# Modulation weighed row by row on VectorE with only partition sums on TensorE, the opening in quarters of 256 features, GpSimd out of both input projections

## Chip, cores and metric

One core of one Trainium2 chip. The metric is the device time of one execution in microseconds; the kernel before takes 3154.66 us (median of three runs, 3153.15 to 3156.14).

## What is computed

Two layers of a diffusion transformer with 1024 latent tokens and 256 context tokens, 1024 features, in f32.

```python
for l in range(DEPTH):                                   # DEPTH = 2
    sh1, sc1, g1, sh2, sc2, g2 = adaln(c, w_mod[l], b_mod[l])         # silu(c) @ w_mod + b_mod, six parts of 1024
    csh1, csc1, cg1, csh2, csc2, cg2 = adaln(c_ctx, w_mod[l], b_mod[l])
    h  = modulate(rms_norm(x, norm1_g[l]), sh1, sc1)                  # h * (1 + scale) + shift
    hc = modulate(rms_norm(xc, norm1_g[l]), csh1, csc1)
    q, k, v, up, ca, cb = project_inputs(h, w_in[l], ...)             # and the same of hc
    attn = diff_attn_post(diff_attention(q, k_all, v_all, lam), ...)  # 4 heads, keys of context and latents
    pool_o = pool_mixer(up, pool_w[l], pool_scale[l])
    conv_o = conformer_conv(ca, cb, ...)                              # depthwise, 31 taps
    mix = jnp.concatenate([attn, pool_o, conv_o], axis=-1)
    x = x + g1 * jnp.einsum('blm,md->bld', mix, w_out[l])
    x = x + g2 * swiglu(modulate(rms_norm(x, norm2_g[l]), sh2, sc2), w_ffn_in[l], w_ffn_out[l])
    if not last:
        xc = ...                                                      # the context, with its own modulation
```

## The kernel before

Features lie on the 128 partitions and tokens along the free dimension, in two blocks of 512 latent tokens and one of 256 context tokens. Every matmul operand is split into two parts (`hi`, rounded by ScalarE, and `lo`, the rest, by VectorE or GpSimd), and each product is three matmuls. `Stream` loads weight tiles ahead of their use and splits them; its argument `lo` says which engine makes the lower parts ("v" VectorE, "p" GpSimd), tile after tile.

A layer is an input projection (14 column tiles, then v), the attention, an output projection and a feed-forward. All DMAs of weights are issued from the SP queue. The order on each engine is that of emission: the main flow emits TensorE's products, and beside it "lanes" (`Kern.lane`) emit smaller work piece by piece, each at a time that a rough forecast (`Clock`) gives. A lane that yields "v-" goes on when the forecast has VectorE idle; so do the convolution's taps (`taps`, 30 adds per 128 channels, besides the centre). What is left of the taps when the attention begins goes on beside it.

The modulation (`adaln`) takes w_mod in tiles of 128 input rows by 512 outputs. Each tile is split, and two matmuls with four columns of the condition (both conditions, in two parts) as weights and the tile as the moving operand add a row of 512 outputs in PSUM; `adaln_end` turns the rows to columns. At the start the tiles of the parts 1 and 0 (scale and shift of the first norm) are loaded whole, every other one is used unsplit in f32, and nothing of the projection begins before both parts are complete. The other four parts of the first layer run on a lane beside the first projection with GpSimd's lower parts; the second layer's six run beside the first feed-forward. GpSimd also adds the squares of the norms (`sq_acc`), makes the pooling sums (`pool_mix`, `POOL_ENG`) and most lower parts of the projections' weights (`P1_LO`), and in the attention the difference of the two softmaxes (`C`).

In the profile, L165 is the line of `Eng` through which every instruction of VectorE, ScalarE, GpSimd and SP goes, and L272 and L277 are TensorE's `mm` and `transpose`; so rows are told apart by tiles: `half` and `part` are tiles of 512 columns, `big` of 1024, `bank` PSUM, `dww` the taps' weights, `mod` the modulation, `cond_st` and `cond_raw` the conditions split and whole, `p`, `st`, `S`, `at` the attention's.

## Time and profile before

| | us |
|---|---|
| median of three runs | 3154.66 |
| span of the profiled execution, first to last instruction | 3148.1 |
| TensorE busy | 2957.6 |
| VectorE busy | 1728.9 |
| GpSimd busy | 1135.8 |
| ScalarE busy | 1098.9 |

The profiled execution has its span alone; the runs' median lies 6.6 us above it. Busy times are unions over one engine's instructions; an engine's idle time counts only where another waits for it.

### The profile page before, as it was taken

How to read it: one execution, taken by the hardware profiler on the slowest of the kernel's cores; microseconds unless marked ns; L12 is line 12 of the kernel's file. 1: busy time of each engine (PE TensorE's matmuls, PEld its weight loads, DVE VectorE, ACT ScalarE, POOL GpSimd, SP SyncE). 2: the span in 40 equal slices, each digit the busy share in tenths (PEclk: the TensorE clock that was granted, in tenths of full speed). 3: DMA queues.
4: the chain of work that ended last, by engine and by line, in shares of the span. 5: the costliest groups of instructions: out<-in, count | busy, mean ns of one | idle time of the engine just before them, and what ended most of it. 6: DMA issues, size and time to landing. Idle time of an engine off the chain costs nothing.

```text
span 3148.1 us, 38069 instructions
## 1 busy us (share of the span) xinstructions
PE 2957.6 (94%) x14708; PEld 2408.0 (76%) x14708; DVE 1728.9 (55%) x2413; ACT 1098.9 (35%) x1892; POOL 1135.8 (36%) x914
## 2 busy tenths in 40 slices
PE   6868898999999999999999998899999999999999
PEld 2646677877777778888888877678877888888887
DVE  5998758985645454332333498869956222322223
ACT  5424536763423332222222233357744111111110
POOL 3655406871423223233332423318832212211221
PEclk9989898999999999999999999999999999999999
DMA  6324364326333232111111222283252111111111
GB/s 229 108 90 122 123 192 140 105 76 203 114 100 95 93 101 81 34 41 41 34 41 40 75 68 70 81 239 95 88 173 75 48 47 54 47 47 47 48 47 54
DMA packets 133188, 283.52 MB, mean 90 GB/s; under 512 B 13840, under 2 KB 47248, under 8 KB 133008
## 3 DMA queue, kind: packets, MB, share of 16 engines
q1 hardware_dynamic: 132720, 280.83, 28.3%
q8 instruction: 116, 1.90, 0.3%
q14 instruction: 64, 0.52, 0.1%
q10 hardware_dynamic: 288, 0.26, 0.0%
HBM read 231.75 MB, written 49.28 MB: 89 GB/s over the span
## 4 chain that ended last, share of the span: by engine, by line
PE 61%; DVE 8%; issue 2%; ACT 1%; POOL 1%; DMA 1%; SPq 0%; DVEq 0%; ACTq 0%; POOLq 0%
PE bank L272 59%; DVE big L165 4%; DVE st L165 2%; DVE half L165 1%; PE S L272 1%; PE bank L277 1%; DVE part L165 1%; DVE at L165 1%; ACT p L165 0%; ACT big L165 0%; POOL p L165 0%; DMA big<-QS 0%; POOL big L165 0%; ACT half L165 0%; DVE rn L165 0%
## 5 line engine op out<-in xcount | busy, mean ns | idle before, releaser
L272 PE MATMUL bank<-part,big 128*128 128x512 f32 (+1 forms) x7536 | 1625.7, 374 | 29.8 <-DVE part L165 9.0
L272 PEld LDWEIGHTS bank<-part,big 128*128 128x128 f32 x7536 | 1321.6, 191 | 310.3 <-DVE part L165 12.9
L165 POOL TENSOR_TENSOR big<-big,big 128x1024 fp32r<-128x1024 f32 (+2 forms) x177 | 431.7, 2450 | 1141.5 <-ACT big L165 850.0
L272 PE MATMUL bank<-half,big 128*128 128x512 f32 (+1 forms) x2640 | 564.5, 373 | 5.4 <-DVE big L165 2.1
L272 PEld LDWEIGHTS bank<-half,big 128*128 128x128 f32 x2640 | 460.0, 188 | 104.4 <-DVE big L165 4.5
L165 DVE TENSOR_TENSOR big<-big,bank 128x512 f32<-128x512 f32 (+1 forms) x130 | 82.7, 679 | 821.4 <-PE bank L272 450.2
L165 DVE SCALAR_TENSOR_TENSOR big<-bank,mod,big 128x512 f32<-128x512 f32 (+1 forms) x560 | 390.4, 736 | 149.9 <-PE bank L272 143.6
L165 ACT CAST big<-big 128x1024 fp32r<-128x1024 f32 (+2 forms) x322 | 298.4, 955 | 68.8 <-DVE big L165 29.8
L165 POOL TENSOR_TENSOR half<-half,half 128x512 fp32r<-128x512 f32 (+2 forms) x141 | 202.7, 1445 | 328.7 <-ACT half L165 298.3
L165 DVE TENSOR_TENSOR big<-big,big 128x1024 fp32r<-128x1024 f32 (+3 forms) x177 | 214.8, 1220 | 188.1 <-ACT big L165 175.4
L165 ACT ACTIVATE big<-bank 128x512 f32<-128x512 f32 x88 | 48.1, 595 | 607.4 <-PE bank L272 607.4
L165 POOL TENSOR_TENSOR big<-big,half 128x256 f32<-128x256 f32 x160 | 124.7, 780 | 289.4 <-ACT half L165 289.4
L165 POOL TENSOR_TENSOR p<-p,p 128x512 f32<-128x512 f32 (+1 forms) x200 | 221.1, 1105 | 16.7
L165 ACT ACTIVATE half<-bank,mod 128x256 f32<-128x256 f32 x160 | 75.8, 474 | 375.1 <-PE bank L272 375.1
L165 DVE TENSOR_REDUCE st<-S 128x1 f32<-128x1280 f32 (+1 forms) x144 | 195.8, 1362 | 12.3 <-PE S L272 12.3
L165 DVE SCALAR_TENSOR_TENSOR big<-big,dww,big 128x1009 f32<-128x1009 f32 (+14 forms) x120 | 200.2, 1701 | 0.5
L165 POOL TENSOR_SCALAR p<-p,st 128x512 f32<-128x512 f32 (+1 forms) x200 | 123.3, 616 | 192.9 <-DVE st L165 150.7
L165 ACT ACTIVATE p<-S,st 128x1280 f32<-128x1280 f32 (+1 forms) x144 | 177.7, 1234 | 39.7 <-DVE st L165 38.0
L272 PE MATMUL S<-kv,big 128*128 128x512 f32 (+1 forms) x672 | 157.7, 370 | 9.6 <-ACT p L165 6.1
L272 PEld LDWEIGHTS S<-kv,big 128*128 128x128 f32 x672 | 120.1, 191 | 37.7 <-ACT p L165 12.3
L272 PE MATMUL bank<-at,kv 128*128 128x256 f32 x960 | 137.5, 290 | 0.0
L165 DVE TENSOR_TENSOR at<-bank,at 128x512 fp32r<-128x512 f32 (+1 forms) x200 | 115.7, 588 | 29.2 <-ACT at L165 25.0
(107 smaller groups left out, 2364.9 us busy)
## 6 DMA issues: line engine op xcount, KB each, us to landing
big<-in_w_ffn_in SPq DMA_DIRECT2D x88, 512.0 KB, 3.6
big<-in_w_mod SPq DMA_DIRECT2D x48, 512.0 KB, 3.8
big<-in_w_ffn_out SPq DMA_DIRECT2D x44, 512.0 KB, 3.7
big<-in_w_out SPq DMA_DIRECT2D x40, 512.0 KB, 4.9
half<-in_w_mod SPq DMA_DIRECT2D x64, 256.0 KB, 3.5
big<-QS SPq DMA_DIRECT2D x128, 128.0 KB, 5.3
big<-in_w_in SPq DMA_DIRECT2D x28, 512.0 KB, 4.8
VS<-big SPq DMA_DIRECT2D x40, 256.0 KB, 3.6
```

The source lines that it names most:

```text
L165: r = fn(*a, **k)
L272: self.tc.nc.tensor.matmul(out, lhsT, rhs, start=start, stop=stop)
L277: self.tc.nc.tensor.transpose(out, in_, ident)
```

## The change

- Modulation: each row of a w_mod tile is multiplied by its condition value (a scalar per partition) and added up over the eight tiles on VectorE in f32 (`weigh`; the first tile of eight on ScalarE); four matmuls with a single column of ones then sum over the partitions and leave columns at once (`column_sums`). The tiles are not split. This holds for both conditions in the parts 4, 3, 5 of the first layer and 1, 0 of the second, for the latents' condition alone in the second layer's other four, and in the opening. Part 2 of the first layer stays with `adaln`.
- Opening: shift and scale come in four quarters of 256 features each. A quarter's tiles hold both (two pieces of 256 columns per row). Once a quarter is weighed, its two feature tiles of the first block are normed, and their products with the four gated column tiles go out, before the next quarter. The context's condition uses f32 matmuls on the same tiles (`open_rows`); quarters 2 and 3 are loaded a second time for it.
- GpSimd: `P1_LO` is ("v",), `POOL_ENG` is "v", and `sq_acc` adds on VectorE.
- Parts 4, 3, 5 of the first layer go from the lane beside the first projection to one that begins with the output projection.

```diff
-P1_LO = ("v", "p", "v") + ("p",) * 11
+P1_LO = ("v",)
-POOL_ENG = "p"
+POOL_ENG = "v"
...
+    def weigh(self, acc, w, k, j):
+        c = self.c4[:, k, j:j + 1]
+        if k == 0:
+            self.act(acc, w, AF.Identity, scale=c)
+        else:
+            self.nc.vector.scalar_tensor_tensor(acc, w, c, acc, ALU.mult, ALU.add)
+
+    def column_sums(self, ps, accs):
+        for j, acc in enumerate(accs):
+            for c in range(4):
+                self.mm(ps[:, 4 * j + c:4 * j + c + 1], acc[:, c * P:c * P + P], self.one, True, True)
...
+    def adaln_v(self, l, chunk, conds, pace, ne=2):
+        st = Stream(self, self.mod_aps(l, [chunk], ne), new=self.half if ne == 1 else self.big, raw_ahead=1)
+        m = self.cp.tile([P, 2, 8], F32, name=self.name("mod"))
+        for n in range(2):
+            accs = [self.half() for _ in range(conds)]
+            for kk in range(KD // ne):
+                w = st.get_raw(KD // ne * n + kk)
+                for e in range(ne):
+                    for j in range(conds):
+                        self.weigh(accs[j], w[:, e, :], ne * kk + e, j)
+                yield pace * ne / 2
+            yield self.pe(*accs)
+            ps = self.bank2()
+            self.column_sums(ps, accs)
...
     def sq_acc(self, acc, x, first):
...
-            self.nc.gpsimd.tensor_tensor(acc, acc, t, ALU.add)
+            self.nc.vector.tensor_tensor(acc, acc, t, ALU.add)
...
-        for _ in self.adaln(0, [1, 0], 0.0, ne=1, whole=True, raw_ahead=RAW):
-            self.adv()
-        self.finish("norm0", "mod")
+        weigh(0, range(KD))
+        ps = columns(0)
+        rows(0)
+        loads(2)
+        weigh(1, range(2))
+        normed(0, ps)
+        ws += [st_in.get(x, 0) for x in range(2)]
+        weigh(1, range(2, KD))
+        ws += [st_in.get(x, 0) for x in range(2, GATED)]
+        outs += [self.bank() for _ in range(GATED)]
+        ps = columns(1)
+        products(0)
+        rows(1)
...
-        self.lane("ada", self.adaln(0, [2, 4, 3, 5], 3.0, ne=1, split_ahead=1, raw_ahead=1, lo=("p",)), ADA_AT)
+            self.lane("ada", self.adaln(0, [2], 3.0, ne=1, split_ahead=1, raw_ahead=1), ADA_AT)
...
+            if not last:
+                for chunk in (4, 3, 5):
+                    self.lane("ada", self.adaln_v(l, chunk, 2, 3.5, ne=1))
...
-            self.lane("ada", self.adaln(l + 1, [1, 0, 2, 4, 3, 5], 5.0, split_ahead=0, raw_ahead=1))
+            for chunk in (1, 0, 2, 4, 3, 5):
+                self.lane("ada", self.adaln_v(l + 1, chunk, 2 if chunk < 2 else 1, 12.0))
```

How the instructions stand now is shown at three places. First GpSimd, from the opening's square sums (`half_133`) to the first projection; before, the squares of the second block and the context and weights' and modulation's lower parts follow:

```order
L165 TENSOR_TENSOR half_133<-half_133,half_155 128x512
L165 TENSOR_TENSOR big_446<-big_443,big_445 128x1024
L165 TENSOR_TENSOR half_134<-half_134,half_473 128x512
L165 TENSOR_TENSOR half_134<-half_134,half_480 128x512
L165 TENSOR_TENSOR half_134<-half_134,half_483 128x512
```

Now, from its constants to the attention's first softmax difference (`p`), GpSimd has only this:

```order
masks.py:199 AFFINE_SELECT ident<-ident 128x128
L163 MEMSET big_1225 128x8 x2
L163 MEMSET big_1230 128x8 x2
L163 MEMSET big_2012 128x8 x2
L163 MEMSET big_2017 128x8 x2
L163 TENSOR_SCALAR p_3143<-p_3143,st_3134 128x256
```

Second VectorE in the opening. Before, the last part of the modulation (`mod_310` is the shift, `mod_158` the scale) stands ahead of the first instruction of the norm (`half_465`):

```order
L165 TENSOR_TENSOR mod_310<-bank_112_390,params 128x2x4
L165 TENSOR_TENSOR mod_310<-bank_112_390,mod_310 128x2x4
L165 TENSOR_TENSOR big_440<-big_437,big_439 128x1024
L165 SCALAR_TENSOR_TENSOR half_465<-big_116,mod_158,half_306 128x512
L165 SCALAR_TENSOR_TENSOR half_468<-big_117,mod_158,half_306 128x512
L165 SCALAR_TENSOR_TENSOR part_405<-half_465,mod_310,part_397 128x512
```

Now the first norm (`half_290`, with the scale `mod_134`) stands behind the first quarter's sums and one weighing of the second quarter (`half_284`), and two weight tiles are split (`big_299`, `big_303`) before the weighing goes on:

```order
L163 SCALAR_TENSOR_TENSOR half_284<-part_202,cond_raw,half_284 128x512
L163 TENSOR_TENSOR mod_133<-bank_62_244,params 128x2
L163 TENSOR_TENSOR mod_134<-bank_62_244,params 128x2
L163 SCALAR_TENSOR_TENSOR mod_134<-mod_134,params 128x2
L163 SCALAR_TENSOR_TENSOR half_290<-big_116,mod_134,half_233 128x512
L163 SCALAR_TENSOR_TENSOR half_293<-big_117,mod_134,half_233 128x512
L163 SCALAR_TENSOR_TENSOR part_168<-half_290,mod_133,part_160 128x512
L163 SCALAR_TENSOR_TENSOR part_169<-half_293,mod_133,part_161 128x512
L163 TENSOR_TENSOR big_299<-big_192,big_298 128x1024
L163 TENSOR_TENSOR big_303<-big_194,big_302 128x1024
L163 SCALAR_TENSOR_TENSOR half_284<-part_204,cond_raw,half_284 128x512
```

Third VectorE in the first attention, between the same two maxima (`TENSOR_REDUCE`) of scores in `S`. Before:

```order
L165 TENSOR_TENSOR big_4346<-big_4104,big_4346 128x256
L165 TENSOR_REDUCE st_4366<-S_4401 128x1
L165 TENSOR_TENSOR at_4409<-bank_1491_4410,at_4408 128x4x128
L165 SCALAR_TENSOR_TENSOR r_1405_3968<-r_1405_3968 128x4
L165 TENSOR_REDUCE st_4445<-S_4433 128x1
L165 TENSOR_TENSOR at_4375<-bank_1495_4440,at_4374 128x4x128
L165 SCALAR_TENSOR_TENSOR rn_4454<-bank_1497_4449,r_1405_3968 128x4
```

Now, with the convolution's taps (`dww`) and the sums and differences of its closing norm (`big_3868`, `big_821`, `big_923`) among them:

```order
L163 TENSOR_TENSOR big_3771<-big_3522,big_3771 128x256
L163 SCALAR_TENSOR_TENSOR big_614<-big_614,dww_597 128x242
L163 SCALAR_TENSOR_TENSOR big_923<-big_622,dww_597,big_923 128x1009
L163 TENSOR_REDUCE st_3791<-S_3826 128x1
L163 TENSOR_TENSOR at_3836<-bank_1115_3837,at_3835 128x4x128
L163 SCALAR_TENSOR_TENSOR r_1018_3385<-r_1018_3385 128x4
L163 SCALAR_TENSOR_TENSOR big_614<-big_614,dww_597 128x241
L163 TENSOR_TENSOR big_3868<-big_821,big_923 128x512
L163 TENSOR_SCALAR big_614<-big_614,dww_597,params 128x256
L163 SCALAR_TENSOR_TENSOR big_614<-big_614,dww_597 128x241
L163 TENSOR_REDUCE st_3877<-S_3860 128x1
```

In the first attention VectorE has 400 instructions between the first and the last matmul with `S`, where it had 321; in the second 281, where it had 253.

## Rows read from the trace of the kernel before

**Rows 1.** The page's first part: the span, then for each engine its busy time in us, its share of the span and its number of instructions.
```profile
span 3148.1 us, 38069 instructions
PE 2957.6 (94%) x14708; PEld 2408.0 (76%) x14708; DVE 1728.9 (55%) x2413; ACT 1098.9 (35%) x1892; POOL 1135.8 (36%) x914
```

**Rows 2.** Busy time by stage: the stretch in us from the span's start and its length, then the busy us and instructions of TensorE, of its weight loads, of VectorE, ScalarE and GpSimd, the clock granted to TensorE (1 is full), the share of the DMA engines and GB/s. The stretches are the opening, the first input projection, the first attention, the first output projection, the first feed-forward, the second projection and the second attention.
```profile
0.00:48.00 48.00, 28.57 (x92) 5.81 (x92) 19.34 (x41) 22.46 (x38) 12.67 (x14) 0.98 0.96 343
48.00:456.00 408.00, 333.88 (x1570) 257.42 (x1571) 337.47 (x439) 167.94 (x322) 191.94 (x119) 0.90 0.37 116
456.00:701.00 245.00, 221.18 (x1397) 192.95 (x1396) 206.33 (x344) 170.18 (x331) 175.73 (x208) 0.94 0.38 110
701.00:838.00 137.00, 127.38 (x644) 105.08 (x642) 75.53 (x87) 53.17 (x75) 42.62 (x28) 0.99 0.55 184
838.00:1809.00 971.00, 966.79 (x4924) 796.41 (x4925) 400.88 (x571) 269.00 (x448) 294.20 (x236) 1.00 0.21 65
1809.00:2104.00 295.00, 261.03 (x1238) 213.45 (x1236) 245.72 (x318) 110.21 (x200) 76.28 (x38) 0.95 0.33 104
2104.00:2301.00 197.00, 182.96 (x1217) 160.61 (x1218) 180.07 (x268) 147.96 (x263) 163.21 (x189) 1.00 0.35 102
```

**Rows 3.** What TensorE waited for from 48 to 456 us: the waiting engine, tile and line, the releaser, us in total, number of waits, the longest.
```profile
PE bank L272 <- DVE big L165: 37.1, 8, 25.8
```

**Rows 4.** The timeline of GpSimd and VectorE from 49 us on: start, length, engine, line, operation, tiles, shapes, number merged into the row.
```profile
49.79 11.65 POOL L165 TENSOR_TENSOR half<-half,half 128x512 f32<-128x512 f32 x7 [3.09 <-ACT half L165]
50.09 1.78 DVE L165 SCALAR_TENSOR_TENSOR half<-big,mod,half 128x512 f32<-128x512 f32 x1
...
62.58 0.74 DVE L165 SCALAR_TENSOR_TENSOR half<-big,mod,half 128x512 f32<-128x512 f32 x1
```

**Rows 5.** The convolution's taps over the whole span, long ones (latent tokens) and short ones (context), by the tile that holds their weights: minimum, median and maximum duration in ns, first and last start.
```profile
L165 DVE SCALAR_TENSOR_TENSOR big<-big,dww,big x120: 1251/1272/3431, 111.9 to 2024.7; 128x1009 f32<-128x1009 f32 x8, 128x1010 f32<-128x1010 f32 x8, 128x1011 f32<-128x1011 f32 x8, 128x1012 f32<-128x1012 f32 x8
L165 DVE SCALAR_TENSOR_TENSOR big<-big,dww x60: 461/474/2610, 143.0 to 436.4; 128x241 f32<-128x241 f32 x4, 128x242 f32<-128x242 f32 x4, 128x243 f32<-128x243 f32 x4, 128x244 f32<-128x244 f32 x4
```

**Rows 6.** The timeline of VectorE and, below it, of GpSimd around 1890 us, in the second projection: runs of long taps, the first without work on GpSimd until 1886.
```profile
1878.76 9.58 DVE L165 SCALAR_TENSOR_TENSOR big<-big,dww,big 128x1018 f32<-128x1018 f32 x8
1888.47 26.20 DVE L165 SCALAR_TENSOR_TENSOR big<-big,dww,big 128x1022 f32<-128x1022 f32 x12
...
1896.57 9.87 POOL L165 TENSOR_TENSOR big<-big,big 128x1024 f32<-128x1024 f32 x3
```

**Rows 7.** Busy time of VectorE in the two projections, of instructions on the taps' weights alone.
```profile
48.00:456.00 408.00, 158.78 (x126) 0.90 0.37 116
1809.00:2104.00 295.00, 93.31 (x62) 0.95 0.33 104
```

**Rows 8.** Groups of instructions from 48 to 456 us, by shape: number, busy us and mean ns of one, then idle time before them; two of GpSimd, one of VectorE.
```profile
L165 POOL TENSOR_TENSOR half<-half,half 128x512 fp32r<-128x512 f32 x64 | 108.5, 1712 | 115.6 <-ACT half L165 89.2 <-DVE big L165 7.2 <-ACT rn L165 6.5
L165 POOL TENSOR_TENSOR big<-big,big 128x1024 fp32r<-128x1024 f32 x13 | 33.5, 2583 | 31.0 <-ACT big L165 23.0 <-issue 7.9
...
L165 DVE TENSOR_TENSOR big<-big 128x512 f32<-128x512 f32 x10 | 13.5, 1365 | 14.6 <-ACT big L165 14.6
```

**Rows 9.** The same kinds on VectorE where GpSimd does nothing: two groups from 2050 to 2100 us, and a single split of 1024 columns at 43 us (a timeline's row).
```profile
L165 DVE SCALAR_TENSOR_TENSOR big<-big,ls,big 128x512 f32<-128x512 f32 x4 | 3.0, 742 | 0.0
L165 DVE TENSOR_TENSOR big<-big 128x512 f32<-128x512 f32 x2 | 1.4, 686 | 0.7 <-ACT big L165 0.7
...
43.28 1.22 DVE L165 TENSOR_TENSOR big<-big,big 128x1024 fp32r<-128x1024 f32 x1
```

**Rows 10.** TensorE's timeline at two places where it doesn't pause: four matmuls of the modulation, and a sum over partitions (four calls), each with the row behind it.
```profile
859.51 1.08 PE L272 MATMUL bank<-big,cond_st 128*4 128x512 f32 x4
860.43 0.75 PE L272 MATMUL bank<-part,big 128*128 128x256 f32 x5
...
755.10 0.95 PE L272 MATMUL bank<-ones,half 128*128 128x1 f32 x8
755.91 1.40 PE L272 MATMUL bank<-part,big 128*128 128x512 f32 x5
```

**Rows 11.** Busy time in two shorter stretches, the middle of the first attention and the first part of the first feed-forward (columns as in rows 2).
```profile
550.00:650.00 100.00, 96.37 (x650) 85.30 (x649) 93.66 (x144) 76.79 (x139) 84.42 (x98) 1.00 0.39 117
840.00:1250.00 410.00, 407.74 (x2067) 323.02 (x2066) 206.44 (x274) 137.97 (x214) 114.16 (x87) 1.00 0.31 94
```

**Rows 12.** Groups from 550 to 650 us: one-element instructions of VectorE, and GpSimd's adds.
```profile
L165 DVE SCALAR_TENSOR_TENSOR st<-st,ls,r 128x1 f32<-128x1 f32 x17 | 6.8, 400 | 0.6
...
L165 POOL TENSOR_TENSOR p<-p,p 128x512 f32<-128x512 f32 x33 | 43.7, 1323 | 2.8
```

**Rows 13.** VectorE's timeline in the first output projection, one weight tile's turn.
```profile
727.51 0.75 DVE L165 SCALAR_TENSOR_TENSOR big<-bank,mod,big 128x512 f32<-128x512 f32 x1 [1.62 <-PE bank L272]
729.90 1.54 DVE L165 TENSOR_TENSOR big<-big,big 128x1024 fp32r<-128x1024 f32 x1 [1.64 <-ACT big L165]
733.07 0.75 DVE L165 SCALAR_TENSOR_TENSOR big<-bank,mod,big 128x512 f32<-128x512 f32 x1 [1.63 <-PE bank L272]
```

**Rows 14.** The opening's timeline: the modulation's loads on the SP queue, and TensorE's first product of the projection.
```profile
5.89 21.64 SPq L165 DMA_DIRECT2D part<-in_w_mod  x32
...
48.11 1.58 PE L272 MATMUL bank<-part,big 128*128 128x512 f32 x2 [5.36 <-ACT part L165]
```

**Rows 15.** The end of the first projection: busy time from 400 to 455 us (columns as in rows 2).
```profile
400.00:455.00 55.00, 54.39 (x265) 44.92 (x264) 35.90 (x81) 21.27 (x47) 2.39 (x1) 1.00 0.59 175
```

More of the change, by code (lines that the diff above doesn't have):

```diff
@@ L406, in adaln_setup, with adaln @@
         self.M = {}
-    def adaln(self, l, chunks, pace, ne=2, whole=False, **kw):
+    def adaln(self, l, chunks, pace, ne=2, **kw):
         nc = self.nc
-        st = Stream(self, self.mod_aps(l, chunks, ne), new=self.part if whole else self.half if ne == 1 else self.big, **kw)
-        i, ready = 0, []
+        st = Stream(self, self.mod_aps(l, chunks, ne), new=self.half if ne == 1 else self.big, **kw)
+        i = 0
         for chunk in chunks:
@@ new lines, in open_aps, with open_rows @@
+    def open_aps(self, c):
+        w = self.io["w_mod"]
+        return [w[0, k * P:(k + 1) * P, 0:2 * D].rearrange("p (s c) -> p s c", s=2)[:, :, c * 256:c * 256 + 256] for k in range(KD)]
+    def open_rows(self, c, ws):
+        ps = self.pm.tile([P, 512], F32, tag="mod", name=self.name("mod"))
+        for k in range(KD):
+            yield self.at(ws(k))
+            self.mm(ps[0:2], self.c4[:, k, 0:2], ws(k), k == 0, k == KD - 1)
+        m2 = self.half()
+        self.nc.scalar.copy(m2[0:2], ps[0:2])
+        yield self.pe(m2)
+        ps = self.bank2()
+        for x in range(4):
+            self.transpose(ps[:, 2 * x:2 * x + 2], m2[0:2, x * P:(x + 1) * P], self.ident[0:2, 0:2])
+        sums = ps[:, 0:8].rearrange("p (x j) -> p j x", j=2)
+        for chunk in range(2):
+            self.mod_part(0, chunk, self.M[0, chunk][:, 1, 2 * c:2 * c + 2], sums[:, 1, 2 * chunk:2 * chunk + 2], 2 * c)
@@ L1264, in run @@
         nc.sync.dma_start(self.params, io["params"])
+        for ch in range(2):
+            self.M[0, ch] = self.cp.tile([P, 2, 8], F32, name=self.name("mod"))
+        shift, scale = (self.M[0, ch][:, 0, :] for ch in range(2))
         acc = [self.half()[:, :w] for w in (512, 512, CTX)]
@@ new lines, in run, with weigh, columns, normed @@
+        sums = [None] * 4
+        def weigh(c, ks):
+            if sums[c] is None:
+                sums[c] = self.half()
+            for k in ks:
+                self.weigh(sums[c], wq[c][k], k, 0)
+        def columns(c):
+            ps = self.bank2()
+            self.column_sums(ps, [sums[c]])
+            return ps
+        lat = [self.new_block(512)]
+        def normed(c, ps):
+            self.mod_part(0, 0, shift[:, 2 * c:2 * c + 2], ps[:, 0:2], 2 * c)
+            self.mod_part(0, 1, scale[:, 2 * c:2 * c + 2], ps[:, 2:4], 2 * c)
+            ks, ts = (2 * c, 2 * c + 1), []
+            for k in ks:
+                ts.append(self.half())
+                nc.vector.scalar_tensor_tensor(ts[-1], xs[k][0], scale[:, k:k + 1], rs0[0], ALU.mult, ALU.mult)
+                self.act(lat[0].hi[k], ts[-1], AF.Identity, bias=shift[:, k:k + 1])
+            for k, t in zip(ks, ts):
+                nc.vector.scalar_tensor_tensor(lat[0].lo[k], t, shift[:, k:k + 1], r32(lat[0].hi[k]), ALU.add, ALU.subtract)
@@ new lines, in rows, with products @@
+        def rows(c):
+            for _ in self.open_rows(c, lambda k: wq[c][k]):
+                pass
+        ws, outs = [], []
+        def products(c):
+            for k in (2 * c, 2 * c + 1):
+                for (hi, lo), o in zip(ws, outs):
+                    self.mm(o, hi[:, k, :], lat[0].hi[k], k == 0, False)
+                    self.mm(o, hi[:, k, :], lat[0].lo[k], False, False)
+                    self.mm(o, lo[:, k, :], lat[0].hi[k], False, k == KD - 1)
+        st_in = self.in_stream(0)
@@ L1281, in run @@
+        rows(1)
+        loads(3)
         for k in range(KD):
             nc.sync.dma_start(xs[k][1], io["xT"][k, :, 512:1024])
-        st_in.load_to(GATED)
+        weigh(2, range(2))
+        normed(1, ps)
+        weigh(2, range(2, KD))
+        ps = columns(2)
+        products(1)
+        weigh(3, range(2))
+        normed(2, ps)
+        weigh(3, range(2, KD))
+        ps = columns(3)
+        products(2)
+        normed(3, ps)
+        products(3)
+        opened = ws, outs
+        del ws, outs, ps, wq, sums, quarter
@@ L1284, in run @@
+        lat.append(self.new_block(512))
+        cxb = self.new_block(CTX)
         xct = [self.big((4, CTX)) for _ in range(2)]
```

79 lines of the change are left out of this document (46 added, 33 removed).

## Prediction

> **What bounds the kernel now.** I read the page first: TensorE is busy 94% of the span [rows 1], so one could think that only matmuls count. The table by stage shows that this holds in some stages only [rows 2]. The first layer's feed-forward (838 to 1809) has TensorE busy 967 of 971 us at full clock: there a matmul taken out is time won. The first input projection (48 to 456) has TensorE busy 334 of 408 us at a mean granted clock of 0.90, and VectorE 337; the second (1809 to 2104) 261 of 295, and VectorE 246. What TensorE waited for in the first one is VectorE above all, 37.1 us in eight waits of which one is 25.8 us long [rows 3]: products of the pooling mixer, whose operand was queued on VectorE behind convolution taps.
>
> Why VectorE is late shows in single instructions. A 128x512 scalar_tensor_tensor took 1.78 us while GpSimd ran its adds, and 0.74 us a little later, when GpSimd had none [rows 4]. The convolution's taps show the same: minimum 1251 ns, median 1272, maximum 3431 [rows 5]; eight in a row with GpSimd idle took 9.58 us (1.20 each), twelve in a row beside GpSimd 26.20 us (2.18 each) [rows 6]. So each engine's work holds up the other's, and the first projection pays for it.
>
> **The change, part by part.** The sum goes by stages, since they have different limits.
>
> *Opening and first projection.* VectorE is busy 19 + 337 = 357 us of the first 456 [rows 2], 78%. Four things change that.
> - GpSimd gets nothing there any more but eight small memsets, so the contention goes. The taps took 158.8 us [rows 7]; 60 long at 1.20 and 60 short at 0.47, with about 3 us for the other six, would be 103: -56. Of the rest, groups such as the ten additions at 1365 ns against 686 [rows 8, 9] give back another 40 or so; that is an estimate, a fifth of the rest's 180 us, where this group gives a half.
> - From GpSimd to VectorE come, at the prices without GpSimd [rows 8, 9]: 16 lower parts of the gate's modulation (0.68 each: 11 us), 13 lower parts of weight tiles (1.22: 16), 21 square sums (13 with the shorter ones), the pooling mixer's sums (14). The weighing of the first two parts adds 28 instructions at 0.74 (21); the 16 splits of modulation tiles on VectorE go (-11). Together +64.
> - 48 modulation tiles (three parts) leave this stage altogether: their 48 GpSimd instructions at 1.7 us [rows 8] and 96 matmuls.
> - The order puts 36 short and 6 long taps and the convolution's end into the attention: 17 + 7.5 + 14, so -38 here.
>
> That leaves VectorE 357 - 56 - 40 + 64 - 38 = 287 us. At today's busy share of 78% the stage that now ends at 456 would end at 367, at 90% at 319; I take about the middle, 346, so **-110 us**. The bounds are -60 (a share of 72%) and -140. TensorE does not undercut that: its 334 us here lose 96 matmuls of 0.23 [rows 10] and part of the low clock. The opening itself I don't count apart. The projection's first product starts at 48.1 now [rows 14]; it needs a quarter of the modulation in place of all of it, so it would start some ten us earlier (an estimate: one weighing of the second quarter stands ahead of the norm on VectorE, and four splits ahead of the products). But each further quarter then costs VectorE seven weighings and four instructions of the norm, some 8 us, so the block's four tiles end only a few us earlier. The quarter tiles come in pieces of 1 KB where 2 KB came. No row of before shows such a load alone; the 32 tiles of before took 21.6 us to issue [rows 14], and at half that pace they would land about 20 us later, which lies inside the bound of -60.
>
> *First attention.* At 550 to 650 VectorE is busy 93.7 of 100 us and GpSimd 84.4, TensorE 96.4 [rows 11]: there is no room. The 38 us that come in are tensor work with two operands in SBUF, beside GpSimd's adds of 1323 ns [rows 12]; instructions of one element take 400 there, so waiting is part of it now. 38 us at least, up to some 60 with waits, against 38 us that VectorE has idle in this stage (245 - 206) [rows 2], most of it in the context's units. I take **+38**, with bounds +15 and +60. Here the Trainium skill speaks against the change. *SBUF — State Buffer*, section "SBUF: two separate sides", says that VectorE with two SBUF inputs and GpSimd take their shared ports as an exclusive lock for a whole instruction, and the loser "fully blocks". The trace agrees in the projections, about one GpSimd add more per instruction [rows 4, 6]. By it every tap in the attention may cost a whole add on either side, and the term would be that of rival 3; by the stage's idle time [rows 2] it is the +38.
>
> *First output projection.* Its VectorE load per weight tile is a split of 1.54 and an update of 0.75 us in 5.56 [rows 13], and 75.5 us of 137 in all [rows 2]. Three parts of the modulation are now weighed from here on: 84 instructions on VectorE (12 more on ScalarE), 62 us, and 12 column sums on TensorE. With the square sums (some 14) VectorE has about 150 us for 137. What is late next is the weight tile's lower part, and TensorE waits. The norm of the first block also takes a run of 14 weighings at once, ahead of itself. I take **+18**, bounds +5 and +35.
>
> *First feed-forward, TensorE's stage.* The next layer's modulation used 192 matmuls in it at 0.92 us for four [rows 10]: -44. In their place come 16 column sums; the same form (four calls, eight passes with one column) took 0.81 us between its neighbours' starts [rows 10]: +13. VectorE's splits (48 of about 1.2 us) become 112 weighings of 0.74 in groups of two to four; VectorE has 206 of 410 us in use there [rows 11], so they hide, but where one falls among the closing products with their updates it delays a bank: +6, an estimate between 0 and 20. **-25**, bounds -33 and -10.
>
> *Second projection.* VectorE 246, less contention (taps 93.3 us [rows 7] against 62 at 1.20, so -19, and some 16 for the rest), plus 14 splits at 1.22, square sums and the pooling sums (about +37), less 17 moved on: 231. At today's share of 83%: 278 for 295, **-18**, bounds -35 and 0.
>
> *Second attention.* Those 17 us arrive where VectorE has 17 of 197 idle [rows 2]: **+10**, bounds 0 and +20.
>
> Sum: -110 + 38 + 18 - 25 - 18 + 10 = -87. The span is 3148.1, so 3061; the three runs' median lies 6.6 above that span, and what lies around the span should stay: **3068 us**. The bounds, taken as independent, make about 40 us either way, and I use 55, since most of them hang on how well VectorE is fed.
>
> **Rivals.**
> 1. *The projections become TensorE's* (0.20). With no contention both stages run at TensorE's pace and the attention's idle takes in the taps: -140, +15, +5, -33, -35, 0: -188, so 2967. For it: from 400 to 455, where GpSimd has 2.4 us of work, TensorE already runs 54.4 of 55 us [rows 15]. Against: VectorE's sum of 287 us is larger than TensorE's.
> 2. *The waits are the order's, not the contention's* (0.12). The long waits come from TensorE's instructions that stand right behind a fresh VectorE result; VectorE with 287 us of work has as long a queue. Then the first projection gives only some 50, the second nothing: -50 + 38 + 18 - 25 + 10 = -9, so 3146. Against: the share of VectorE's time that is mere waiting is too large.
> 3. *The attention pays it all back* (0.08): slower. 107 instructions more stand on VectorE in the two attentions, some 70 of them with both inputs in SBUF. If each waits out an add of 1.3 us and holds GpSimd in turn for 0.7, that is 140 us on top of the work of 55; with the other stages as above (-135) the kernel comes to about +60: 3215. It decides from the point where the attentions lose more than 135 us together. For it: the one-element instructions of 400 ns [rows 12]. Against: while TensorE, VectorE and GpSimd take turns, part of such waiting falls into idle time.
>
> **How the numbers follow.** My forecast has 0.60, and its own range is 3013 to 3123. Measured runs lie within 0.05% of their median here, and 0.2% (6 us) is about what a measurement can tell from no change. Faster: all of the forecast and of rival 1, half of rival 2: 0.86; same 0.05; slower 0.09. The range goes down halfway into rival 1 and up to the time of rival 2: 2980 to 3146.
>
> **What would show it.** In the table by stage: the attention's start at 320 to 395 us instead of 456; GpSimd empty before it; taps with a maximum close to their minimum there. In the attention, taps of up to 2.5 us, and a stage of 260 to 300 us. In the output projection, TensorE's waits for splits. In the feed-forward, column sums in place of the modulation's matmuls and some 25 us less. I am wrong if the first projection keeps more than 350 us, if the attention grows by over 60, or if TensorE begins to wait in the feed-forward.

## The result and the profile after

The changed kernel takes **3196.41 us** (median of four runs, 3192.67 to 3197.35) against 3153.9 (median of four) for the kernel before on the same chip: a ratio of 1.0139, 95% interval 1.0124 to 1.0153. It is slower by 43 us; 3068 was forecast, with 3146 as the upper end.

The page of the profile begins:

```profile
span 3194.4 us, 37668 instructions
PE 2962.2 (93%) x14604; PEld 2437.1 (76%) x14604; DVE 1786.4 (56%) x2734; ACT 1044.3 (33%) x1806; POOL 804.5 (25%) x715
```

Busy time by stage, with the columns of [rows 2]. A stage is cut here at TensorE's first product of it; the last row is the second attention. The cuts of [rows 2] lie up to 8 us from this one (456 where it gives 463 for the kernel before, 1809 for 1817, 2301 for 2308).

```profile
0.00:49.40 49.40, 16.46 (x48) 7.84 (x49) 24.23 (x47) 15.80 (x23) 0.70 (x6) 0.88 1.01 342
49.40:388.00 338.60, 314.88 (x1521) 243.93 (x1522) 255.29 (x439) 126.92 (x243) 0.54 (x8) 0.96 0.36 112
388.00:702.40 314.40, 247.64 (x1402) 211.47 (x1401) 248.26 (x422) 193.21 (x365) 180.17 (x208) 0.85 0.29 88
702.40:880.60 178.20, 147.64 (x735) 120.26 (x733) 130.70 (x195) 55.24 (x81) 15.20 (x6) 0.91 0.62 215
880.60:1869.20 988.60, 953.72 (x4875) 800.28 (x4875) 458.46 (x678) 238.96 (x425) 280.65 (x225) 0.99 0.21 65
1869.20:2116.70 247.50, 246.28 (x1146) 202.51 (x1147) 204.06 (x297) 90.16 (x166) 0.28 (x4) 0.98 0.37 114
2116.70:2359.10 242.40, 206.85 (x1297) 179.79 (x1296) 200.65 (x303) 169.30 (x293) 169.36 (x192) 0.94 0.28 87
```

The projections are shorter and GpSimd is empty there; the second is TensorE's now: it is busy in 246 of 247.5 us. The first attention takes 314 us and no engine is full in it. In the output projection VectorE has 131 us of work where it had 75.5 [rows 2], and the granted clock is 0.91. The feed-forward is no shorter.

All stages below are cut in this way, in us (opening to the projection's first product; first projection to the first product into `S`; and so on); "rest" is the second layer's output projection and feed-forward. The stages are those of the one profiled execution, the last column is the median of the runs; the two lie up to 6 us apart, so a stage's difference of a few us says little.

| kernel | opening | in 1 | attn 1 | out 1 | ffn 1 | in 2 | attn 2 | rest | median |
|---|---|---|---|---|---|---|---|---|---|
| before | 48 | 415 | 238 | 135 | 982 | 285 | 206 | 840 | 3154 |
| after | 49 | 339 | 314 | 178 | 989 | 247 | 242 | 835 | 3196 |
| e1 convolution first | 49 | 385 | 241 | 178 | 990 | 276 | 212 | 838 | 3167 |
| e2 no tables | 48 | 338 | 292 | 179 | 990 | 247 | 229 | 834 | 3161 |
| e3 no taps | 49 | 338 | 275 | 179 | 990 | 243 | 240 | 834 | 3152 |
| e4 no closing | 49 | 341 | 270 | 180 | 991 | 246 | 211 | 834 | 3123 |
| e5 parts back | 48 | 461 | 241 | 133 | 982 | 281 | 208 | 835 | 3191 |
| e6 squares GpSimd | 48 | 384 | 240 | 183 | 966 | 278 | 212 | 841 | 3157 |
| e7 matmuls, layer 2 | 50 | 384 | 243 | 179 | 1008 | 272 | 211 | 833 | 3181 |
| e8 GpSimd back | 54 | 392 | 238 | 186 | 960 | 288 | 208 | 837 | 3169 |
| e9 opening back | 47 | 352 | 241 | 180 | 991 | 275 | 211 | 834 | 3132 |
| e10 no weighing | 49 | 385 | 242 | 154 | 984 | 280 | 207 | 835 | 3132 |
| e11 plain f32 | 49 | 407 | 241 | 136 | 964 | 277 | 211 | 840 | 3127 |
| e12 e11 + opening | 49 | 368 | 244 | 138 | 964 | 276 | 211 | 837 | 3088 |
| e13 GpSimd out alone | 49 | 397 | 240 | 136 | 1006 | 276 | 211 | 836 | 3154 |
| e14 e12 + GpSimd | 48 | 393 | 243 | 136 | 961 | 285 | 207 | 838 | 3116 |
| e15 layer 2 weighed alone | 49 | 412 | 240 | 137 | 960 | 286 | 208 | 839 | 3132 |

### The profile page after: what moved, and what is told of

Same layout as the page of the kernel before. It is cut to its first block, busy times and chain, and to the rows that moved or that the text cites. A ratio compares the mean times of both kernels' runs of the same rounds, so it can differ in the third digit from the quotient of the medians.

```text
span 3194.4 us, 37668 instructions
## 1 busy us (share of the span) xinstructions
PE 2962.2 (93%) x14604; PEld 2437.1 (76%) x14604; DVE 1786.4 (56%) x2734; ACT 1044.3 (33%) x1806; POOL 804.5 (25%) x715
## 4 chain that ended last, share of the span: by engine, by line
PE 73%; DVE 14%; ACT 5%; issue 3%; DMA 3%; POOL 1%; SPq 0%; ACTq 0%; DVEq 0%; POOLq 0%
PE bank L270 68%; DVE big L163 5%; DVE half L163 3%; DVE st L163 3%; PE S L270 3%; PE bank L275 2%; ACT p L163 1%; ACT big L163 1%; DVE at L163 1%; ACT half L163 1%; PE mod L270 1%; DMA part<-in_w_mod 1%; ACT L313 1%; DVE rn L163 1%; DVE part L163 1%
## 5 line engine op out<-in xcount | busy, mean ns | idle before, releaser
L163 POOL TENSOR_TENSOR big<-big,big 128x1024 fp32r<-128x1024 f32 x137 | 331.8, 2438 | 1107.5 <-ACT big L163 875.4
L270 PE MATMUL bank<-half,big 128*128 128x512 f32 (+1 forms) x2640 | 573.1, 375 | 16.8 <-DVE big L163 7.9
L163 ACT ACTIVATE big<-bank 128x512 f32<-128x512 f32 x88 | 48.1, 595 | 660.5 <-PE bank L270 660.5
L163 ACT CAST big<-big 128x1024 fp32r<-128x1024 f32 (+2 forms) x274 | 250.3, 938 | 39.6 <-DVE big L163 27.3
L163 POOL TENSOR_TENSOR p<-p,p 128x512 f32<-128x512 f32 (+1 forms) x200 | 222.5, 1112 | 16.7
L270 PE MATMUL S<-kv,big 128*128 128x512 f32 (+1 forms) x672 | 176.7, 404 | 40.3 <-ACT p L163 36.2
L163 DVE TENSOR_TENSOR big<-big,big 128x1024 fp32r<-128x1024 f32 (+5 forms) x169 | 159.1, 953 | 54.4 <-ACT big L163 52.1
L270 PEld LDWEIGHTS S<-kv,big 128*128 128x128 f32 x672 | 133.1, 212 | 73.7 <-ACT p L163 43.7
L163 DVE SCALAR_TENSOR_TENSOR big<-big,dww,big 128x1009 f32<-128x1009 f32 (+14 forms) x120 | 150.1, 1277 | 0.4
L275 PE MATMUL bank<-ident,p 128*128 128x128 f32 x656 | 113.8, 296 | 33.2 <-DVE big L163 10.6
```

Source lines behind the costliest of these rows:

```text
L163: r = fn(*a, **k)
L270: self.tc.nc.tensor.matmul(out, lhsT, rhs, start=start, stop=stop)
L275: self.tc.nc.tensor.transpose(out, in_, ident)
```

## The experiments

**The attention.** The theory: score (TensorE), maximum (VectorE), exponential (ScalarE) and the next score take turns, and what the convolution left behind stands in the queues of these engines: its taps, and its closing (a norm and an activation, for which ScalarE loads another function table). Four kernels part it: in e1 all of it is moved ahead, in e2 the function tables are left out, in e3 the taps, in e4 the closing.

e1:
```diff
+            self.finish("conv0", "conv1", "convc")
             self.attention(l, not last, early, out_soon)
```


> The changed kernel, with what is left of the convolution (taps, closing norm, activation) emitted ahead of each attention instead of beside it. In the changed kernel the first attention (first product into S to the first product of the output projection) takes 314 us where 238 were taken before, the second 242 where 206. Theory Q (the attention is a chain score - maximum - exponential through the in-order queues of VectorE and ScalarE, and whatever of the convolution stands in these queues lengthens it): the attentions fall back to about 238 and 206; the two projections end 40 to 60 and 20 to 30 us later, since some 38 and 17 us of VectorE work lie bare there; 3140 to 3175 us in all. Rival C (the attention is slow for another reason: its earlier start, the low clock of TensorE from the context's units, the loads of keys and queries): the first attention stays above 280, and the kernel comes to 3210 or more.

e2, inside the attentions:
```diff
+        if self.attn and func == AF.Silu:
+            func, want = AF.Identity, None
```


> The changed kernel, with the convolution's closing activation replaced by a plain scale and bias inside the attentions, so that ScalarE needs no other function table there: the 12 and 8 table loads of 1.28 us each are gone, everything else stands as before (part of the computation is changed). Rival T (it is the table loads in ScalarE's queue that hold up the exponentials): the attentions lose 40 us or more of the 76 and 36 that they gained. Theory Q: at most the loads' own 15 and 10 us, so 3172 to 3190.

e3:
```diff
-            if s == 0:
+            if s == 0 or self.attn:
                 continue
```


> The changed kernel without the taps that fall inside the attentions (42 and 4; this work is left out), the closing norm stays there. Theory Q: the first attention falls by the taps' 36 us of VectorE or a little less, to 275 to 285, the second by 5; 3150 to 3165. If the closing norm is what counts: first attention still above 295, 3175 to 3195. If it is VectorE and GpSimd shutting each other out: more than 36, the first attention below 270.

e4, in `conv_end`:
```diff
+            if self.attn:            # split x0, x1, write them
+                ...
+                continue
             nc.vector.tensor_tensor(t, x0, x1, ALU.add)
```


> The changed kernel, where the convolution's closing norm and activation are left out inside the attentions (only the two-part split and the writing remain), the taps stay there. Theory Q: the closing norm stands in the queues with its waits for TensorE and ScalarE and its table loads, so the first attention falls by 30 to 45 us and the second by 25 to 35; 3115 to 3145. If only the taps' work counts: less than 15 in each, 3175 or more.

Measured: 3167, 3161, 3152 and 3123. e1 brings the attentions back to 241 and 212 and the projections up by 46 and 28: rival C falls. TensorE's waits for exponentials in the first attention, 25.8 us in 23 waits in the changed kernel, are 4.6 us in 13 in e1. Without taps the first attention becomes 39 us shorter, without the closing 44, and the second 3 and 31. So the taps and the closing account for the loss: in the first attention each for about half (39 and 44 overlap, as e1 takes away 73), in the second nearly all of it is the closing. e2 takes 22 and 13 us, more than the loads' own 15.4 and 10.3 and less than rival T's 40. Those loads, busy time of ScalarE in the two attentions of the changed kernel:

```profile
388.00:703.00 315.00, 15.40 (x12) 0.85 0.29 88
...
2110.00:2362.00 252.00, 10.26 (x8) 0.94 0.31 95
```

How it goes shows in the timeline of the changed kernel. ScalarE loads a table, does one activation of the closing, loads the table back, and only then makes the exponential; TensorE's next score has waited 3.68 us for it. VectorE stands 3.82 us before a result of TensorE that the closing norm wants, and GpSimd 12.40:

```profile
507.91 1.28 ACT L313 ACT_TABLE_LOAD   x1
...
509.20 0.82 ACT L163 ACTIVATE big<-big,params 128x512 f32<-128x512 f32 x1
...
510.69 1.28 ACT L313 ACT_TABLE_LOAD   x1
...
511.99 1.33 ACT L163 ACTIVATE p<-S,st 128x1280 f32<-128x1280 f32 x1
...
513.46 2.50 PE L270 MATMUL S<-kv,big 128*128 128x512 f32 x6 [3.68 <-ACT p L163]
...
522.32 1.29 DVE L163 SCALAR_TENSOR_TENSOR big<-bank,big 128x512 f32<-128x512 f32 x2 [3.82 <-PE bank L270]
...
525.50 0.69 POOL L163 TENSOR_SCALAR p<-p,st 128x512 f32<-128x512 f32 x1 [12.40 <-DVE st L163]
```

The six products into `S` took 2.50 us there behind the pause and 1.33 at 507.30, behind none; the granted clock is 0.50 from 513.4 to 516 and 1.00 from 507 to 509 (1.2 and 2.4 GHz). e1, the two attentions without these visitors, with TensorE busy 217 us in the first one where it was 248, at a mean clock of 0.92 where it was 0.85:

```profile
434.20:675.50 241.30, 216.99 (x1367) 188.98 (x1366) 207.05 (x347) 171.35 (x335) 175.76 (x208) 0.92 0.35 101
2118.60:2330.60 212.00, 196.60 (x1271) 171.62 (x1270) 187.75 (x279) 155.08 (x274) 165.84 (x192) 0.96 0.31 94
```

**Output projection, feed-forward, GpSimd**, each on top of e1.

e5:
```diff
-            self.lane("ada", self.adaln(0, [2], 3.0, ...), ADA_AT)
+            self.lane("ada", self.adaln(0, [2, 4, 3, 5], 3.0, ...), ADA_AT)
...
-                for chunk in (4, 3, 5):
-                    self.lane("ada", self.adaln_v(l, chunk, 2, 3.5, ne=1))
```


> The kernel of e1_conv_first (3167; convolution finished ahead of the attentions), with the modulation's parts 4, 3, 5 of the first layer back beside the first projection as split tiles and matmuls. Theory W (the 43 us that the first output projection lost come from the weighing beside it): the output projection falls from 178 to 135 to 145 us and the feed-forward by up to 5; the first projection grows from 385 by 20 to 45 (48 splits of 0.69 on VectorE, 96 matmuls of 0.23). 3140 to 3165. If the output projection's loss is from the square sums on VectorE: it stays above 160, and the kernel comes to 3175 or more.

e6, in `out_proj` and the closing of `ffn`:
```diff
-            self.nc.vector.tensor_tensor(acc, acc, t, ALU.add)
+            self.nc.gpsimd.tensor_tensor(acc, acc, t, ALU.add)
```


> The kernel of e1_conv_first, with the square sums of the output projections and of the feed-forward's closing products back on GpSimd (the opening's and the first projection's stay on VectorE). If the square sums on VectorE matter: the first output projection falls by 10 to 25 us (13 and 8 sums of 0.69 leave a queue in which the weight tiles' lower parts wait), the end of the first feed-forward by 8 to 15: 3130 to 3150. Theory W: less than 8 in the output projection; 3150 to 3165.

e7:
```diff
-                self.lane("ada", self.adaln_v(l + 1, chunk, 2 if chunk < 2 else 1, 12.0))
+            self.lane("ada", self.adaln(l + 1, [1, 0, 2, 4, 3, 5], 5.0, split_ahead=0, raw_ahead=1))
```


> The kernel of e1_conv_first, with the second layer's modulation in the first feed-forward as before: split tiles and 192 matmuls in place of 112 weighings and 16 column sums. By TensorE's work alone (44 us against 13) the feed-forward grows from 989 to about 1020, and the kernel to 3190 to 3200. If the waits that the weighing brings into the feed-forward eat its gain: 980 to 997, 3157 to 3175.

e8: `P1_LO` and `POOL_ENG` as before, all of `sq_acc` on GpSimd.

> The kernel of e1_conv_first, with GpSimd back at all its work in the projections: lower parts of the weights, pooling sums, all square sums. Theory of the contention (what stands on VectorE beside GpSimd takes longer by more than the work that moves): the first projection grows from 385 to 410 to 425, the second from 276 to 285 to 295, the output projection and the feed-forward's end fall by some 15 in all: 3175 to 3205. If the projections are held up by VectorE's queue and not by the contention: first projection at most 390, second at most 280, the kernel 3140 to 3160.

Measured: 3191, 3157, 3181 and 3169. e5: without the weighing the output projection takes 133, so theory W holds for it; but beside the first projection the parts cost 76, not 20 to 45 (TensorE waited 64.9 us for VectorE's `big` tiles, 34.7 in one piece; the tiles' lower parts, on GpSimd before the change, are VectorE's here), so the kernel became slower, against the expectation. e6: nothing in the output projection (it grew by 5), but 23 us in the feed-forward, more than expected. e7: 18 us, between the two expectations. e8: 2 us in all; 7 and 12 more in the projections, 8 in the output projection and 5 in the opening, 30 less in the feed-forward. So little in the projections speaks against the contention; but in both e1 and e8 the convolution's rest lies bare at the end of the first projection (TensorE is busy 8.5 and 17.3 of its last 30 us), which can hide the rest: the 126 instructions on the taps' weights take 104 us in e1 and 117 in e8. e13 and e14 ask again.

Why the square sums count in the closing products (VectorE's timeline, changed kernel): update, square on ScalarE, addition, and only then the next update, 2.1 us a round; the norm behind it starts late.

```profile
1846.25 0.69 DVE L163 TENSOR_TENSOR half<-half,half 128x512 f32<-128x512 f32 x1 [0.76 <-ACT half L163]
1846.86 0.75 DVE L163 SCALAR_TENSOR_TENSOR big<-bank,mod,big 128x512 f32<-128x512 f32 x1
1848.36 0.69 DVE L163 TENSOR_TENSOR half<-half,half 128x512 f32<-128x512 f32 x1 [0.76 <-ACT half L163]
```
TensorE's row behind it:
```profile
1865.84 1.08 PE L275 MATMUL bank<-ident,rn 128*128 128x128 f32 x4 [9.18 <-DVE rn L163]
```

**Opening, weighing, and a better kernel.**

e9, on e1: the opening's code as before the change, square sums on VectorE, part 2 of the modulation put off by 60 us instead of 25.

> The kernel of e1_conv_first, with the opening as before the change (modulation's parts 1 and 0 whole, every other tile split, matmuls; all four gated column tiles behind the complete norm), square sums still on VectorE; part 2 of the modulation starts 35 us later on its lane. In the changed kernel the last gated column tile's activation starts at 160 us, in the kernel before at 134. If the opening in quarters costs these 26 us: the first attention starts at 405 to 415 instead of 434, the kernel takes 3139 to 3148. If VectorE's queue in the projection is the limit, so that an earlier opening is lost again: attention from 425 on, 3158 to 3167.

e10, on e1:
```diff
+                        if l or ne * kk + e == 0:
                             self.weigh(accs[j], w[:, e, :], ne * kk + e, j)
```


> The kernel of e1_conv_first, with the 84 weighings on VectorE of the parts 4, 3, 5 beside the first output projection left out (their loads, ScalarE's 12 first weighings and the column sums stay; part of the computation is left out). If VectorE's work there is what costs the output projection its 43 us: it falls from 178 to 135 to 148, the kernel takes 3115 to 3130. If it is the 48 loads of 256 KB, which share the SP queue and the DMA engines with the output weights: it stays above 165, the kernel above 3150.

e11, on e6, `adaln` for the parts 2, 4, 3, 5 beside the first projection, no `adaln_v` in this layer (the tiles stay whole, and one f32 matmul takes the place of two):
```diff
-                        self.mm(ps[0:4], self.S[:, k, :], hi[:, e, :], k == 0, False)
-                        self.mm(ps[0:4], self.S[:, k, :], lo[:, e, :], False, k == 7)
+                        self.mm(ps[0:4], self.c4[:, k, :], w[:, e, :], k == 0, k == 7)
```


> The kernel of e6_squares_gpsimd (3157), with the modulation's parts 2, 4, 3, 5 of the first layer beside the first projection as single f32 matmuls on unsplit tiles: no weighing, no split, 64 matmuls with four columns of about 0.6 us (the opening's 16 took 9.65). If TensorE has room for them in its waits there: the first projection grows from 384 by 15 to 35 us, the output projection falls to 133 to 140, the feed-forward by up to 7: 3125 to 3145. If the projection is TensorE's by now and pays all of them: it grows by 40 or more, 3150 to 3165.

e12, on e11, with the opening of e9:

> The kernel of e11_plain_f32 with the opening as before the change, its square sums and the first projection's on GpSimd as before: left of the change are the weights' lower parts and the pooling sums on VectorE and the second layer's weighing. If the opening's cost and the first layer's weighing add up as single edits: 20 to 28 us below e11, 3100 to 3122. If they overlap: 3125 to 3140.

Measured: 3132, 3132, 3127 and **3088** (ratio 0.9802, interval 0.9788 to 0.9817). e9: the quarters cost 35 us, more than the 26 expected. e10: 24 us in the output projection and 6 in the feed-forward are VectorE's weighing; the projection stays 20 above e5's 133, between the two expectations. TensorE's time on sums over partitions is 14.7 us there and 2.8 in e5, so the column sums can make some 12 of the 20; the rest (loads, ScalarE's weighings) is left open. e11: as expected, +23 in the first projection and -47 in the output projection. e12 takes 38 us less than e11, below its expected range. It beats both kernels.

Where the quarters lose: VectorE, changed kernel. Ahead of the norm of the first and second quarter stands the sum for the context's condition, which waits for TensorE:

```profile
36.01 0.23 DVE L163 TENSOR_TENSOR mod<-bank,params 128x2 f32<-128x2 f32 x2 [12.67 <-PE bank L275]
...
37.47 1.42 DVE L163 SCALAR_TENSOR_TENSOR half<-big,mod,half 128x512 f32<-128x512 f32 x2
...
65.67 0.23 DVE L163 TENSOR_TENSOR mod<-bank,params 128x2 f32<-128x2 f32 x2 [15.83 <-PE bank L275]
```
and TensorE is at the f32 rows of that condition, then at column sums whose operand VectorE has not weighed yet:
```profile
25.25 9.65 PE L270 MATMUL mod<-part,cond_raw 128*2 128x512 f32 x16
...
47.72 1.84 PE L270 MATMUL bank<-ones,half 128*128 128x1 f32 x8 [11.74 <-DVE half L163]
```
The last gated tile's activation then starts at 160 us, here, and in e9 at 125:
```profile
160.42 0.38 ACT L163 ACTIVATE half<-bank 128x256 f32<-128x256 f32 x1 [4.28 <-PE bank L270]
```
```profile
124.90 0.38 ACT L165 ACTIVATE half<-bank 128x256 f32<-128x256 f32 x1 [4.06 <-PE bank L272]
```

And the output projection of the changed kernel. VectorE waits 6.10 us for a modulation tile; the SP queue takes 26 us over nine of them; a run of 14 weighings stands ahead of the norm; TensorE waits for the sums behind it:

```profile
774.05 2.74 DVE L163 SCALAR_TENSOR_TENSOR half<-half,cond_raw,half 128x512 f32<-128x512 f32 x4 [6.10 <-DMA half<-in_w_mod]
...
775.50 26.06 SPq L163 DMA_DIRECT2D half<-in_w_mod  x9
...
793.17 9.36 DVE L163 SCALAR_TENSOR_TENSOR half<-half,cond_raw,half 128x512 f32<-128x512 f32 x14
...
802.01 3.55 PE L270 MATMUL bank<-ones,half 128*128 128x1 f32 x16 [9.88 <-DVE half L163]
```

**The change's parts alone.** e13 is the kernel before with `P1_LO`, `POOL_ENG` and `sq_acc` as changed, and e1's edit. e14 is e12 with `P1_LO` and `POOL_ENG` as before. e15 is the kernel before with e7's lane reversed, `adaln_v` for the second layer.

> The kernel before with one part of the change alone: weights' lower parts, pooling sums and square sums on VectorE instead of GpSimd (the modulation's lower parts stay on GpSimd), and the convolution finished ahead of the attentions, where it stood before too. If the contention costs more than the work that moves to VectorE (the prediction's first term without the modulation): the first projection falls from 415 to 375 to 395, the second from 285 to 265 to 275: 3105 to 3135. If VectorE's queue pays for the work as it did for GpSimd's: first projection 415 to 440, the feed-forward's end up by 20 as in the changed kernel: 3155 to 3195.

> The kernel of e12_opening_plain (3088), with the weights' lower parts and the pooling sums back on GpSimd. Here no modulation tile is split in the first projection, so the two runs differ by GpSimd's share alone. By the contention theory the first projection grows from 368 by 20 to 35 and the second from 276 by 8 to 15: 3115 to 3140. If what the contention costs and what the moved work costs are about equal: 3080 to 3100.

> The kernel before with one part of the change alone: the second layer's modulation weighed on VectorE in the first feed-forward, square sums on GpSimd. By the predicted term (-31 of TensorE's work, +6 of waits) and by e7_mod1_matmul (18): the first feed-forward falls from 982 to 957 to 965 and the kernel to 3126 to 3136. If the weighing disturbs the feed-forward even without square sums on VectorE: 970 or more, 3140 to 3150.

Measured: 3154, 3116 and 3132. e14: with GpSimd in the projections the kernel takes 28 us more; the first is 25 us longer and the second 9. e13: the projections gain 18 and 9, near the contention theory's 20 to 40 and 10 to 20, and the feed-forward's end takes back 24 through the square sums, so the whole stays where it was. e15: -21 in the feed-forward, near the -25 forecast. The first projection of e12, and below it that of e14 (columns as in [rows 2]):

```profile
48.50:416.30 367.80, 357.19 (x1601) 242.60 (x1602) 277.24 (x473) 136.99 (x260) 16.88 (x22) 0.99 0.41 130
```
```profile
47.60:440.70 393.10, 366.73 (x1601) 248.71 (x1602) 288.23 (x440) 136.67 (x259) 80.39 (x55) 0.96 0.39 122
```

VectorE has 33 instructions fewer in e14 and is busy 11 us longer. Without GpSimd TensorE is busy 97% of the stage at a clock of 0.99. In e12 and e14 the convolution's rest does not lie bare: TensorE is busy through the last 30 us before the attention. The taps' instructions alone, e12 and then e14 (158.78 us before, [rows 7]; the stretch of e14 ends at 435, with all 126 in it):

```profile
48.00:416.00 368.00, 102.19 (x126) 0.99 0.41 130
```
```profile
48.00:435.00 387.00, 121.20 (x126) 0.95 0.39 121
```

## Why the prediction was wrong

| term | forecast | measured |
|---|---|---|
| opening and first projection | -110 | -75 |
| first attention | +38 | +77 |
| first output projection | +18 | +43 |
| first feed-forward | -25 | +7 |
| second projection | -18 | -38 |
| second attention | +10 | +37 |
| rest | 0 | -4 |

Two of the three signs of being wrong came: the first attention grew by more than 60, and TensorE waits in the feed-forward (9.2 us in one piece at its end). The first projection kept 339 us, under the 350.

- **The contention was right.** The taps' longest instruction is 1695 ns where it was 3431, and most come near their least price (before: [rows 5, 7]):
```profile
L163 DVE SCALAR_TENSOR_TENSOR big<-big,dww,big x120: 1260/1273/1695, 137.9 to 2134.4; 128x1009 f32<-128x1009 f32 x8, 128x1010 f32<-128x1010 f32 x8, 128x1011 f32<-128x1011 f32 x8, 128x1012 f32<-128x1012 f32 x8
```
  The sum for VectorE held too: it is busy 280 us in the opening and the first projection, where 287 were forecast. e14 prices GpSimd's share at 28 us. Rival 2 (the order, not the contention) does not explain that: the same 126 instructions took 102 us in e12 and 121 in e14. One reading was loose: in [rows 4] an instruction beside GpSimd took 1.04 us more, not a whole add (11.65 us for seven, 1.66 each).
- **"The opening itself I don't count apart"** failed. It was called some ten us early at its start and a few at its end, with 20 us of later loads "inside the bound of -60". Its first product came at 49.4 instead of 48.1, and e9 gives 35 us. By that price the term without the quarters would be about -110, as forecast (an estimate: e9 stands on e1, not on the changed kernel). What was overlooked stands in the change itself: the context's f32 rows and the column sums go into TensorE's queue ahead of the products, and their results into VectorE's ahead of the norm. The rows above show the waits (12.67 and 15.83 us); how the 35 us split between them, the rows' own 16.7 us on TensorE and the tiles loaded twice, no run shows.
- **"38 us at least, up to some 60 with waits, against 38 us that VectorE has idle"** failed. The VectorE time was about right (248 us against 206, so +42), but the idle time was not free: it is the turn of ScalarE and TensorE in a chain. And only VectorE's share of the convolution's closing was counted (14 us); its activations and 12 table loads on ScalarE, and its waits for TensorE in VectorE's queue, were not. By e4 the closing is 44 of the 77, in the second attention 31 of 37. Of the first projection's 75 us gained and the second's 38, e1 shows that 46 and 28 were only moved into the attentions.
- **Output projection, +18 with +35 as the upper bound**, measured +43: the weighings are 24 of it (e10). The 12 column sums were named and given no price; some 12 us of TensorE's time are theirs. The square sums, put at 14 us of VectorE, made no difference here (e6). And "a run of 14 weighings at once, ahead of itself" was seen and not priced. It takes 9.4 us, TensorE waits 9.9 behind it, and the mean clock from 775 to 800 is 0.77. VectorE's work was forecast as 150 us for 137 and is 131 for 178: not a full engine, but a queue in which a split stands behind a weighing that waits for its tile.
- **Feed-forward, -25**: the weighing's term was right (e15: -21; e7: 18). The square sums on VectorE, which I priced in the projections and the output projection but not here, cost 23 us at the end of this stage (e6; e13: 24), and the first layer's weighing another 6 (e10). Together that is +8, for the +7 measured.
- **Rival 3** had the right side and place (the attentions lost 113 together, it needed 135 with the other terms as forecast), but not the right mechanism: it made each added instruction wait out an add of GpSimd. In the first attention the 43 instructions on the taps' weights took 30.1 us, where their medians make 25.2 (36 of 0.478, 6 of 1.266, one of 0.4): 5 us of such waiting, for a loss of 77. GpSimd's 208 instructions took 180 us there and 176 in e1: 4 us more. The Trainium skill's rule cited in the prediction is thus seen in the trace, at a small part of the price.
- **Rival 1** came true where it could: the second projection is TensorE's (246 of 247.5), and so is the first from 163 us on (220 of 225).

On the table changes the Trainium skill, *ScalarE: Activation LUTs*, section "What ACT_TABLE_LOAD costs", gives 1283 ns for the load and 2.66 us for a whole switch. The trace has loads of 1.28 us; e2 took away 20 of them and gained 35 us, 1.76 each. The page's 2.66 is not seen here: in the rows above, the load from 507.91 ends at 509.19, and the activation behind it starts at 509.20.

## What to carry to other kernels

Idle time of an engine in a stage where engines take turns was not room here: 30 us of taps cost 39, and the closing 44. What is put into a queue there can lengthen the turn, and so can a function-table change on ScalarE. When a stage gets shorter, ask first what has left it and where that now stands; e1 took one line. Price a moved operation in every stage where it runs (the square sums stand in four), and at each place where a new product's operand is made late, since TensorE's queue waits too.

## What the runs showed of the hardware

- A plain f32 matmul took TensorE twice as long as the two matmuls on a split tile. With four columns of the condition as weights and 512 columns of an unsplit tile moving, one call of the code leaves two records in the trace (64 calls in e12, 128 records) and took 0.95 us, from the start of the two to the next row's start; the two calls on a split tile take 0.46 [rows 10]. (So the 16 records of 9.65 us that e11's expectation counts are eight calls.) e11 pays that: TensorE is busy 384 us in the first projection where it was 326 in e6. But the stage grew by 23 us only, since TensorE had idle time there; in return no tile is split and none is weighed beside the output projection, which is 47 us shorter.

```profile
200.16 1.02 PE L272 MATMUL mod<-half,cond_raw 128*4 128x512 f32 x2
201.11 1.65 PE L272 MATMUL bank<-part,big 128*128 128x512 f32 x6
```
```profile
L272 PE MATMUL mod<-half,cond_raw 128*4 128x512 f32 x128 | 65.9, 599 | 1.6 <-ACT half L165 1.6
```

- Where TensorE waited, it also ran at a lower clock. In the output projection before the change it was busy 23.4 of 25 us from 775 to 800 with the full clock granted (1 is 2.4 GHz). In the changed kernel the mean over the same 25 us is 0.77, and 13 us of work are done: behind the wait of 4.59 us that ends at 779 the granted clock is 0.51 (1.2 GHz) from 780 to 785, with TensorE busy throughout, then 1.00, and 0.50 again from 795 to 805, in and behind the wait of 9.88 us that ends at 802. At the end of the changed kernel's attention, where no convolution is left, it is at 1.00 again.

```profile
650.00:703.00 53.00, 48.07 (x335) 42.66 (x335) 45.99 (x71) 36.96 (x70) 41.59 (x48) 1.00 0.02 5
775.00:800.00 25.00, 12.99 (x53) 10.12 (x53) 19.02 (x32) 8.00 (x11) 0.00 (x0) 0.77 0.47 161
```
